# Low probabilities of a head's first 512 queries: from pairs of 64-column products to full products

## The chip, the core and the metric

The kernel runs on one core of a Trainium2 chip. The core has a matrix engine, TensorE (PE in the profile, with its weight loads shown as a row of their own, PEld), and four others: VectorE (DVE), ScalarE (ACT), GpSimd (POOL) and SyncE (SP), which here issues the DMAs. The metric is the time of one execution on the device, in microseconds (us); less is better. Beside the runs that are timed there is one execution taken by the profiler, from which all rows of the trace come.

## The reference

Two decoder layers over 1024 tokens of width 1024. Layer 0 mixes by causal pooling, layer 1 by attention with forget gates over 16 heads of 64 channels; both also attend to 256 memory tokens with 4 heads. The part that matters here is the attention of layer 1:

```python
def forgetting_attention(u, k, v, cum):
    ...
        logits = jnp.einsum('bqhd,bkhd->bhqk', qi, k,
                            preferred_element_type=jnp.float32) * scale
        logits = logits + (ci[..., :, None] - cum_k[:, :, None, :])
        ...
        logits = jnp.where(mask[None, None], logits, -jnp.inf)
        p = jax.nn.softmax(logits, axis=-1)
        return jnp.einsum('bhqk,bkhd->bqhd', p.astype(v.dtype), v)
```

All of it is float32. A query sees the keys up to its own place only, so with blocks of 128 the query block i needs i + 1 blocks of keys.

## The kernel before

TensorE is fed in 16-bit types or in a rounded form of float32, and the kernel keeps the accuracy by splitting numbers into a high and a low part. Products are then made of three: high with high, high with low, low with high. For the attention's values both probabilities and V are in float16: V of a head is stored as 128 columns for each block of 128 keys, 64 of its high part and 64 of its low part, and the probabilities, transposed, as one 128 x 128 block for each block of keys and part.

**fox()** runs the attention. Its outer loop goes over the 16 heads, two to a pair, its inner loop over the 8 blocks of 128 queries of a head, from the longest (i = 7) to the shortest. Each step does the following.

- `probs` (lines up to L1000): the products of queries and keys go to PSUM (written through the helper `mm3`, L231, into a bank of tag "L", of which there are 3). DVE adds the forget terms and keeps the running extreme (L986); POOL masks the diagonal block first (L978). ACT takes the exponential into a bank of tag "T", of which there are 2 (L994).
- `inverse_of` (L1004 to L1007): DVE forms one over the sum of a row.
- `halves` (L1015, L1016): ACT writes the high part of the scaled probabilities, DVE the low part.
- `turn` (L1028): a DMA on SP's queue transposes both parts into a tile of tag "T" in SBUF.
- `values` (L1034 to L1058): some steps later, once for the query blocks 4 to 7 (c = 1) and once for the blocks 0 to 3 (c = 0) of each head, the products with V. All four blocks of queries share one PSUM bank of 512 columns (tag "O", a single one).

Between these the helper `Fill` pumps in the products of other work (projections and gates of pairs to come: `slab`, L253, with PSUM banks of tag "pj"; toward the end the first part of the output projection, L540). How much is pumped where is counted in columns and shared out by step.

In `values`, the list `blocks` holds the pairs of a query block i and a key block j: 8 + 7 + 6 + 5 = 26 for c = 1, 4 + 3 + 2 + 1 = 10 for c = 0. A first loop (L1045) multiplies the 128 columns of V, high and low, with the high probabilities: rows 0 to 63 of the bank collect V's high part, rows 64 to 127 its low part. A second loop (L1051) multiplies V's high 64 columns alone with the low probabilities, by turns into the upper and the lower half of the bank, so that two successive products stand on different 64 columns of the array. At the end ACT (L1057) scales one half of the bank into the output tile and DVE (L1058) adds the other half, so it is the sum of both halves that counts, whichever half a term went to.

PE's instructions run in the order of the program, which is written out by hand (`tc.manual_schedule(engines={PE})`). The order on ACT, DVE, POOL and SP's queue is set by a planner when the kernel is built. It goes by modelled times and by what is ready; the program pins a few places with `tc.issue_after` and `tc.keep_in_program_order`.

After the last head, `out_proj.rest` (L540, with the splitting of its weights and inputs on ACT and DVE in `hi_lo`, L189 to L196) and the layer norm end the kernel.

Of the kernel before, what the change touches and what calls it, by code (L numbers as in the profile page):

```python
# [99 lines left out]
def trunk_kernel(ctx, tc, x, xT, memT, win, wk, wv0, wv, wmk, wmv, wout, poolw, pscale, lng, lnb, bforget, out):  # L100
# [5 lines left out]
    nc = tc.nc  # L106
# [22 lines left out]
    def ps(shape, tag, bufs):  # L129
        return psum.tile(shape, F32, tag=tag, name=nm(tag), bufs=bufs)  # L130
# [241 lines left out]
    def mem_attention(l, XH, XL, kv, qtile, ytile, yd):  # L372
# [85 lines left out]
        if True:  # L458
            for t in range(ST + 2):
                part = fill.left / (5 * (ST + 2 - t))  # L460
                if t < ST:
                    probs(t)
                fill.pump(part if t <= ST else 3 * part)
                for h in range(MH):
                    if t >= 3 and t % 2 == 1:
                        values((t - 3) // 2, h)
                    fill.pump(part if t <= ST else part / 2)
            fill.pump(float("inf"))
# [287 lines left out]
    with tc.tile_pool(name="in1", bufs=1) as in1:  # L756
# [262 lines left out]
        pt, homes = {}, {}  # L1019
# [14 lines left out]
        def values(hd, c, o):  # L1034


            (v, un), b = pairs[hd // 2][2], hd % 2
            acc = ps([P, NH], "O", 1)
            blocks = [(i, j) for i in range(4 * c + 3, 4 * c - 1, -1) for j in range(i + 1)]

            def cols(i):
                return slice((i % 4) * P, (i % 4 + 1) * P)

            for n, (i, j) in enumerate(blocks):
                nc.tensor.matmul(  # L1045
                    acc[:, cols(i)], v[:, b, 2 * j : 2 * j + 2, :].rearrange("p e d -> p (e d)"), pt[hd, i][:, j, :],
                    start=n == 0, stop=False, skip_group_check=True,
                )
            for n, (i, j) in enumerate(blocks):
                half = slice(64 * (n % 2), 64 * (n % 2) + 64)  # L1050
                nc.tensor.matmul(  # L1051
                    acc[half, cols(i)], v[:, b, 2 * j, :], pt[hd, i][:, i + 1 + j, :],
                    start=False, stop=n >= len(blocks) - 2, skip_group_check=True,
                )
            own, other = slice(64 * b, 64 * b + 64), slice(64 - 64 * b, P - 64 * b)
            oc = o[own, c * NH : (c + 1) * NH]
            nc.scalar.activation(oc, acc[other, :], AF.Copy, scale=un[own])  # L1057
            return nc.vector.scalar_tensor_tensor(oc, acc[own, :], un[own], oc, ALU.mult, ALU.add).ins  # L1058
# [30 lines left out]
        def fox(following, out_proj):  # L1089
# [8 lines left out]
            for hd in range(HEADS + 1):  # L1098
# [20 lines left out]
                for i in range(ST if hd < HEADS else LAG):  # L1119
# [46 lines left out]
                    if older and older[1] == (4 if older is past[0] else 0):  # L1166
                        last = values(older[0], older[1] // 4, older[2])
                        out_proj.behind = last if older[1] else out_proj.behind
                        if older[0] % 2 and older[1] == 0:
                            finished = pair_out(older[0] // 2, older[2], gs.get(older[0] // 2))  # L1170
# [83 lines left out]
```

## Time and profile before

| what | us |
|---|---|
| median of 3 runs | 1199.49 |
| lowest and highest run | 1198.80, 1199.53 |
| the profiled execution | 1198.79 |
| its span, first to last instruction | 1197.0 |
| mean granted clock of TensorE, share of full speed | 0.999 |

How to read the rows further down. A row of a source line gives the kind of instruction, the tiles (written <- read), a count, and durations as least, median and greatest in ns. A row of the timeline gives the start in us from the span's start, the length of the group in us, engine, line, operation, tiles, shapes, count, and in square brackets how long the engine was idle before it and what it was waiting for. A row of waits gives the engine and line that waited, the one that released it, the total in us, how often, and the longest. The engine named as releaser is inferred from the order of events; "issue" means that the profile shows nothing that was waited for. Ends of products on PE are modelled by the profiler, starts are recorded, and a product's recorded length contains its passage through the array, in which the next ones have already begun. A few per cent of the records of products can be missing.

### The profile page before, as it was taken

Reading aid. Unit: us, or ns where it says so; the run is one execution under the profiler, and the core shown is the slowest. Engines: PE = TensorE matmul, PEld = TensorE weight load, DVE = VectorE, ACT = ScalarE, POOL = GpSimd, SP = SyncE. Lnnn points to the kernel's source line nnn. Section 1 sums busy time; section 2 is a strip of 40 time slices with the busy share of each in tenths; the row PEclk is TensorE's granted clock in tenths of the full one; section 3 lists DMA queues with packets and bytes.
Section 4 is the critical chain, followed back from the end, with each engine's and each line's share of the span. In section 5 each row is a group of like instructions: output and inputs, shape, how many; then the busy total and the mean of one; then the engine's idle time right before and its main releaser. Section 6 shows DMA issues by size and latency. Waiting matters only on the chain. (4 is left out here: it accounts for less than half of the span.)

```text
span 1197.0 us, 19472 instructions
## 1 busy us (share of the span) xinstructions
PE 1172.2 (98%) x6810; PEld 739.3 (62%) x6927; DVE 800.5 (67%) x1864; ACT 616.9 (52%) x1330; POOL 208.4 (17%) x312
## 2 busy tenths in 40 slices
PE   9999999999999999999999999999999999999997
PEld 4567665555555555677776666666666666655554
DVE  6544767374656576377546888778878888874654
ACT  7433654262532224366325777767766787773110
POOL 2000000000000000200103334333334324530000
PEclk9999999999999999999999999999999999999999
DMA  7333654242355666355526789879897999976431
GB/s 246 115 101 87 131 115 159 79 123 80 102 197 158 159 156 161 106 138 100 171 54 161 152 199 173 195 155 195 187 186 164 195 191 210 230 206 229 154 116 48
DMA packets 280803, 182.06 MB, mean 152 GB/s; under 512 B 225024, under 2 KB 238976, under 8 KB 280704
## 3 DMA queue, kind: packets, MB, share of 16 engines
q1 hardware_dynamic: 280704, 180.81, 62.0%
q8 instruction: 54, 0.88, 0.3%
q14 instruction: 45, 0.37, 0.1%
HBM read 95.24 MB, written 22.61 MB: 98 GB/s over the span
## 5 line engine op out<-in xcount | busy, mean ns | idle before, releaser
L253 PE MATMUL pj<-A,w 128*128 128x512 bf16 (+1 forms) x1817 | 571.4, 398 | 2.2 <-DVE B L894 1.1
L253 PE MATMUL pj<-A,wl 128*128 128x512 bf16 x929 | 351.8, 380 | 6.4 <-issue 3.4
L253 PEld LDWEIGHTS pj<-A,w 128*128 128x128 f32 x944 | 174.8, 188 | 45.4 <-POOL wl L200 2.0
L253 PEld LDWEIGHTS <-w 128*128 128x128 bf16 x960 | 93.1, 98 | 121.3 <-issue 39.4
L253 PEld LDWEIGHTS <-wl 128*128 128x128 bf16 x960 | 94.3, 98 | 87.9 <-issue 4.2
L994 ACT ACTIVATE T<-MK,s 128x512 f32<-128x512 f32 x192 | 111.0, 578 | 44.5 <-DVE s L986 22.6
L1015 ACT ACTIVATE P<-T,s 128x512 f16<-128x512 f32 x192 | 103.1, 576 | 52.8 <-issue 26.3
L1016 DVE SCALAR_TENSOR_TENSOR P<-T,s,P 128x512 f16<-128x512 f32 x192 | 112.3, 612 | 24.0 <-ACT P L1015 22.3
L540 PEld LDWEIGHTS <-T 128*128 128x128 bf16 x736 | 70.6, 98 | 88.9 <-issue 6.8
L190 DVE TENSOR_TENSOR wl<-raw,w 128x512 bf16<-128x512 f32 (+1 forms) x96 | 67.9, 713 | 72.3 <-ACT w L189 69.7
L231 PE MATMUL L<-B,B 128*128 128x512 f32 (+3 forms) x384 | 109.0, 386 | 4.6 <-DVE s L986 4.2
L189 ACT CAST w<-raw 128x512 fp32r<-128x512 f32 (+1 forms) x104 | 62.8, 609 | 84.0 <-PE pj L253 57.6
L231 PEld LDWEIGHTS L<-B,B 128*128 128x128 f32 x384 | 71.1, 189 | 29.6 <-DVE s L986 9.9
L353 POOL TENSOR_SCALAR A<-A 128x1024 bf16<-128x1024 f32 x8 | 8.4, 1049 | 444.5 <-ACT A L351 427.9
L986 DVE CUSTOM_DVE_ANT_0 MK<-L,R 128x512 f32<-128x512 f32 (+3 forms) x128 | 72.8, 569 | 8.4 <-PE L L231 5.6
L978 POOL TENSOR_SCALAR_AFFINE_SELECT R<-R 128x128 f32<-128x128 f32 x128 | 42.2, 335 | 207.4 <-DVE s L986 162.5
L200 POOL TENSOR_TENSOR wl<-raw,w 128x512 bf16<-128x512 f32 x54 | 69.4, 1285 | 3.8
L190 DVE TENSOR_TENSOR T<-T,T 128x1024 bf16<-128x1024 f32 x23 | 31.6, 1374 | 48.1 <-ACT T L189 48.0
L189 ACT CAST T<-T 128x1024 fp32r<-128x1024 f32 x23 | 24.1, 1047 | 71.7 <-DMA T<-y1d 45.4
L199 POOL TENSOR_SCALAR w<-raw 128x512 fp32r<-128x512 f32 x54 | 35.9, 665 | 58.5 <-PE pj L253 58.5
L540 PE MATMUL L<-B,T 128*128 128x512 bf16 (+1 forms) x163 | 43.1, 391 | 0.3
L433 ACT ACTIVATE P<-L,s 128x256 f32<-128x256 f32 x64 | 29.6, 474 | 23.4 <-issue 13.0
(296 smaller groups left out, 1789.7 us busy)
## 6 DMA issues: line engine op xcount, KB each, us to landing
raw<-in_win_dram SPq DMA_DIRECT2D x94, 256.0 KB, 2.9
raw<-in_wout_dram SPq DMA_DIRECT2D x40, 256.0 KB, 2.9
B<-B SPq DMA_DIRECT2D x32, 256.0 KB, 4.5
R<-cumd SPq DMA_DIRECT2D x16, 512.0 KB, 4.6
T<-y0d SPq DMA_DIRECT2D x12, 512.0 KB, 5.1
y0d<-Y SPq DMA_DIRECT2D x11, 512.0 KB, 2.7
T<-y1d SPq DMA_DIRECT2D x11, 512.0 KB, 4.7
raw<-in_wmk_dram SPq DMA_DIRECT2D x16, 256.0 KB, 2.7
```

The costliest lines, as they stand in the source:

```text
L189: pin(nc.scalar.copy(hi, src))
L190: pin(by.tensor_tensor(lo[0], src, hi.bitcast(F32), ALU.subtract))
L199: nc.gpsimd.tensor_scalar(hi, src, 1.0, 1.0, ALU.mult, ALU.mult)
L200: nc.gpsimd.tensor_tensor(lo[0], src, hi.bitcast(F32), ALU.subtract)
L231: nc.tensor.matmul(acc, a, b, start=i == 0, stop=i == len(terms) - 1)
L253: nc.tensor.matmul(acc, a, b, start=start, stop=stop)
L540: nc.tensor.matmul(acc, y, w, start=c == 2 and j == firsts[id(acc)] and acc is not self.seeded, stop=c == 1 and j == lasts[id(acc)], skip_ ...
L978: nc.gpsimd.affine_select(R[:, qs], R[:, qs], [[-1, P]], ALU.is_ge, -NEG, base=0, channel_multiplier=1).ins
L986: nc.vector.tensor_tensor_reduce(p[:, lo:up], lg, R[:, lo:up], 1.0, top, ALU.add, ALU.min, m[:, n : n + 1])
L994: nc.scalar.activation(e, p[:, lo:up], AF.Exp, bias=top, scale=-1.0, accum_out=sums[:, n, hd % 2, i : i + 1],)
L1015: nc.scalar.activation(pair[:, lo:up], e, AF.Copy, scale=r)
L1016: nc.vector.scalar_tensor_tensor(pair[:, L + lo : L + up], e, r, pair[:, lo:up], ALU.mult, ALU.subtract)
```

## The change

For c = 0 the second loop takes V's high and low columns together, 128 of them, in place of the high 64 by turns on two halves of the array. Its products have the form of the first loop's, and the bank's closing mark is set on the last of them alone. For c = 1 nothing changes. The number of products is the same, 10 in each loop. The sum gains a term that was left out before, low probabilities with V's low part.

```diff
-            for n, (i, j) in enumerate(blocks):
+            if c == 0:
+                for n, (i, j) in enumerate(blocks):
+                    nc.tensor.matmul(
+                        acc[:, cols(i)], v[:, b, 2 * j : 2 * j + 2, :].rearrange("p e d -> p (e d)"),
+                        pt[hd, i][:, i + 1 + j, :], start=False, stop=n == len(blocks) - 1, skip_group_check=True,
+                    )
+            for n, (i, j) in enumerate(blocks if c else ()):
                 half = slice(64 * (n % 2), 64 * (n % 2) + 64)
                 nc.tensor.matmul(
                     acc[half, cols(i)], v[:, b, 2 * j, :], pt[hd, i][:, i + 1 + j, :],
```

## The prediction

> **What bounds the kernel now.** I read the page first: which engine is full, and by how much.
>
> ```profile
> span 1197.0 us, 19472 instructions
> PE 1172.2 (98%) x6810; PEld 739.3 (62%) x6927; DVE 800.5 (67%) x1864; ACT 616.9 (52%) x1330; POOL 208.4 (17%) x312
> ```
>
> TensorE (PE) is busy for 98% of the span. Time taken from it ought to come off the end, unless something else is as full where the change sits. So I asked for the busy time of the stretch in which the attention heads run, with the columns stretch, length, and busy time and count of PE, weight loads, DVE, ACT and POOL, then granted clock, DMA share and GB/s.
>
> ```profile
> 660.00:1060.00 400.00, 389.04 (x2629) 256.59 (x2674) 327.26 (x938) 292.68 (x679) 155.66 (x249) 1.00 0.92 188
> ```
>
> PE works 389 of these 400 us, DVE 327. That says PE. But the waits say something else. First what PE waited for from 655 to 1075 us, then what DVE waited for from 660 to 1060 (total, times, longest):
>
> ```profile
> PE L L231 <- DVE s L986: 4.2, 9, 1.0
> PE pj L253 <- issue: 3.8, 24, 0.2
> PE pj L253 <- DVE B L894: 1.1, 2, 0.5
> ```
>
> ```profile
> DVE P L1016 <- ACT P L1015: 22.0, 39, 1.1
> DVE s L1004 <- ACT T L994: 21.6, 25, 1.6
> DVE MK L986 <- PE L L231: 1.4, 4, 0.4
> ```
>
> DVE and ACT hand the softmax to and fro: DVE waits 22.0 and 21.6 us for ACT in these two groups, and only 1.4 us, in 4 places, for PE's logits (L231). PE in turn is held 9 times by DVE's reading of the logits (L986) and twice by DVE's reading of a projection (L894). So two chains run side by side, PE's and that of DVE with ACT, and each is sometimes ahead. Where in time they hold each other decides what a saving on PE is worth; that comes below.
>
> **The change, part by part.** It touches values() for c = 0 alone: 10 products with the low probabilities per head, 16 heads, 160 of the 576 products on L1051. All instances by shape:
>
> ```profile
> L1045 PEld LDWEIGHTS <-V x576: 96/98/100, 663.4 to 1069.0; 128*128 128x128 f16 x192
> L1045 PE MATMUL O<-T,V x576: 219/219/230, 663.6 to 1069.1; 128*128 128x128 f16 x192
> ```
>
> ```profile
> L1051 PEld LDWEIGHTS <-V x576: 106/110/110, 665.2 to 1069.4; 128*64 128x64 f16 x192
> L1051 PE MATMUL O<-T,V x576: 219/219/243, 665.2 to 1069.5; 128*64 128x128 f16 x192
> ```
>
> A product's 219 ns are its passage through the array; products overlap, so only spacings of starts count. The first c = 0 burst, the last but one, and for comparison a c = 1 burst (start, length of the group, product, count, idle before):
>
> ```profile
> 673.70 0.72 PE L1045 MATMUL O<-T,V 128*128 128x128 f16 x10
> 674.36 0.47 PE L1051 MATMUL O<-T,V 128*64 128x128 f16 x10
> 674.99 0.38 PE L253 MATMUL pj<-A,wl 128*128 128x512 bf16 x1 [0.16 <-issue]
> ...
> 1045.37 0.72 PE L1045 MATMUL O<-T,V 128*128 128x128 f16 x10
> 1046.02 0.47 PE L1051 MATMUL O<-T,V 128*64 128x128 f16 x10
> 1046.65 0.38 PE L253 MATMUL pj<-A,w 128*128 128x512 bf16 x1 [0.16 <-POOL R L1083]
> ```
>
> ```profile
> 663.63 1.61 PE L1045 MATMUL O<-T,V 128*128 128x128 f16 x26
> ```
>
> Removed: the halves. Ten of them are cheap in themselves: (0.47 - 0.22) / 9 = 28 ns from start to start, two of them in the time of one full product, which is (1.61 - 0.22) / 25 = 55.6 ns in the burst of 26. What is dear is getting in and out. The tenth full product starts at 673.70 + 9 x 0.0556 = 674.20, the first half only at 674.36: 0.16 us instead of 0.056, so 0.10 lost. The last half starts at 674.36 + 0.47 - 0.22 = 674.61, and the next ordinary product at 674.99: 0.38 us, where PE shows 0.16 idle after the half has left the array. The burst takes 674.99 - 673.70 = 1.29 us in all, 1.28 in the last but one; 15 of the 16 bursts have this form.
>
> The tiling page of the Trainium skill (TensorEngine Tiling (Array Packing), Key Properties) says that a change of tiling mode drains the array. The trace agrees: 0.10 us going in and 0.38 coming out.
>
> Added: 10 full products, so 20 in a row on one shape. Another place of this kernel has such a run without any halves behind it:
>
> ```profile
> 565.63 0.83 PE L231 MATMUL T<-T,MK 128*128 128x128 f16 x12
> 566.30 0.38 PE L253 MATMUL pj<-A,w 128*128 128x512 bf16 x1
> ```
>
> Twelve take 566.30 - 565.63 = 0.67 us up to the start of the next ordinary product, 55.8 ns each and nothing lost behind them. Twenty take 20 x 55.8 = 1.12 us. Against 1.28 that is 0.165 us less per burst (between 0.16 and 0.18 by 55.6 to 55.8 ns and 1.28 to 1.29 us), for 15 bursts 2.5 us. The loads of 128 columns (98 ns) are hidden already: the burst of 26 has one ahead of each product and still goes at 55.6. Dependences, counts of instructions, DMAs and tiles stay as they are, and the fill between the bursts is counted in columns that the change doesn't touch.
>
> The sixteenth burst is followed by f32 products that start before the halves have left:
>
> ```profile
> 1068.55 0.73 PE L1045 MATMUL O<-T,V 128*128 128x128 f16 x10
> 1069.21 0.47 PE L1051 MATMUL O<-T,V 128*64 128x128 f16 x10
> 1069.61 0.50 PE L540 MATMUL pj<-MK,B 128*128 128x512 f32 x1
> ```
>
> There it is 1.06 us before and 1.12 after; I take it as 0, with -0.06 as the bound.
>
> Moved: the sum in PSUM is finished later within a burst, at 19 x 0.0556 + 0.22 = 1.28 us after its start instead of 0.66 + 0.47 = 1.13. ACT reads it next (L1057); the burst with the least time between is this (PE, then ACT):
>
> ```profile
> 889.23 0.47 PE L1051 MATMUL O<-T,V 128*64 128x128 f16 x10
> ```
>
> ```profile
> 890.05 0.69 ACT L1057 ACTIVATE G<-O,unscale 64x512 f32<-64x512 f32 x1
> ```
>
> Before, the sum is there at 889.70, 0.35 ahead of ACT; 0.15 later still leaves 0.2. I cost it at nothing. Without that cover ACT's queue, with the next exponentials (L994) in it, would start up to 0.15 later.
>
> **Where the 2.5 us go.** Here are the places in time where PE is held by DVE, and then those where DVE's reading of the logits is held by PE.
>
> ```profile
> 687.66 0.62 PE L231 MATMUL L<-B,B 128*128 128x384 f32 x2 [0.83 <-DVE s L986]
> 749.96 0.47 PE L253 MATMUL pj<-A,w 128*128 128x512 f32 x1 [0.53 <-DVE B L894]
> 827.60 0.38 PE L231 MATMUL L<-B,B 128*128 128x256 f32 x1 [0.41 <-DVE s L986]
> 857.83 0.47 PE L253 MATMUL pj<-A,w 128*128 128x512 f32 x1 [0.53 <-DVE B L894]
> 1075.32 0.38 PE L540 MATMUL L<-MK,T 128*128 128x512 bf16 x1 [0.54 <-DVE MK L190]
> ```
>
> ```profile
> 780.12 0.69 DVE L986 CUSTOM_DVE_ANT_0 MK<-L,R 128x512 f32<-128x512 f32 x1 [0.28 <-PE L L231]
> 796.29 0.69 DVE L986 CUSTOM_DVE_ANT_0 MK<-L,R 128x512 f32<-128x512 f32 x1 [0.43 <-PE L L231]
> 887.96 0.69 DVE L986 CUSTOM_DVE_ANT_0 MK<-L,R 128x512 f32<-128x512 f32 x1 [0.25 <-PE L L231]
> 904.13 0.69 DVE L986 CUSTOM_DVE_ANT_0 MK<-L,R 128x512 f32<-128x512 f32 x1 [0.43 <-PE L L231]
> ```
>
> Follow the time. DVE with ACT sets the pace up to 749.96, where PE last waits for it. From there PE sets it, until DVE is short of logits at 780.12 and 796.29. Then DVE again, up to 857.83; PE up to 904.13; and from 904.13 on DVE isn't short of logits once, until PE waits at 1075.32 for weights that DVE splits. A PE that is 0.165 us early in a stretch that DVE paces only waits longer at that stretch's end. In PE's two stretches lie four bursts (751.65, 780.73, 859.53, 888.58): there the saving shortens DVE's waits of 0.28, 0.43, 0.25 and 0.43, which are larger than the 0.165 or 0.33 that arrives. Four times 0.165 is 0.66 us; the other eleven, 1.8 us, turn into waits on L986, L894 and L190.
>
> The profiled execution took 1198.79 us (its span of 1197.0 and 1.8 around it), 0.70 below the median of the runs, 1199.49. So 1198.79 - 0.66 = 1198.13 against the profiled one, and 1198.8 against the median. A measurement of this kernel can tell about 0.2%, 2.4 us, from no change, so this is no change.
>
> **Rivals.** All of the saving counts: PE is at 98%, the DVE waits at these places are short, and DVE's order in the stretch may have its own slack, a shorter PE giving it projections (L894, L905) earlier. Against it: DVE waits for PE in four places only. 1199.49 - 2.5 = 1197.0, or 0.21% faster, on the border of what can be told.
>
> The order on the other engines changes. PE's order is written out by hand, that of DVE, ACT, POOL and the DMA queue is worked out when the kernel is built, by a planner that goes by modelled times. If it prices full products unlike halves, near ties flip, and an operation put ahead of L1004 or L1016 makes DVE wait once more for ACT. The row of L1004 gives 21.6 / 25 = 0.86 us for such a wait. It decides where DVE paces, some 12 heads; one more in half of them costs 6 x 0.86 = 5.2, less 0.66: 1204.0. It takes four such waits (3.4 us) to be slower by more than can be told. For it: DVE is busy for 327 of 400 us there, and 25 waits of this kind stand already. Against it: same number of instructions and columns. The same flips could fall well: two waits less, with the 2.5, give 1195.3.
>
> Full products go at the pace of their loads: 98 ns instead of 55.8, 20 x 98 = 1.96 us a burst, 0.68 more than now, for 15 bursts 10.2: 1209.7. The burst of 26 at 55.6 is against it. The Trainium skill (TensorE: Matmul & The Clock Gate, Back-to-back issue gap) gives about 81 ns a product for a stream of pairs of load and product on 128 columns; by it 20 would take 1.62 us, 0.34 more than now, 16 x 0.34 = 5.4 in all, an estimate of 1204.9. This trace shows 55.6 for the same thing, and that decides.
>
> **How the numbers follow.** Forecast (part of the saving counts, order as before): 0.42. All of it counts: 0.20. Order changes: 0.36, of which 0.22 to the slower side, 0.14 to the faster. Pace of the loads: 0.02. Faster takes two thirds of the second case (0.14), the good flips (0.14) and a little of the forecast in which more bursts count than I found (0.08): 0.36. Slower is 0.22 and 0.02: 0.24. The rest, 0.40, is within 0.2%. The range goes from the good flips, 1195.3, to the bad ones, 1204.0; the forecast's own is 1197.0 to 1199.5.
>
> **What would show it.** In the changed profile a c = 0 burst should be one group of 20 products on 128 columns, 1.12 us to the next start, with no idle of 0.16 behind it; if it is near 1.6 or 2, the loads set the pace. DVE's waits for PE's logits should fall from 1.4 us, and PE's waits for L986 and L894 rise from 5.3 by about 1.8. If these stay and the span falls by 2.5, PE paced everywhere. If DVE's operations stand in another order around L1004, L1016 and L1058, the planner has moved, and the time is that of the new order. I am wrong if the time leaves 1197.0 to 1199.5 with the order unchanged.

## The result, and the profile after

The changed kernel takes 1201.61 us (median of 15 runs, 1200.93 to 1203.59) against 1199.39 for the kernel before beside it (15 runs, 1198.46 to 1199.91): a ratio of 1.0021, with a 95% interval from 1.0014 to 1.0029. That is 2.2 us slower: little, but the interval is clear of 1. The profiled execution took 1201.12 us.

The page of the kernel after, the span and the busy time of the engines:

```profile
span 1199.3 us, 19478 instructions
PE 1174.5 (98%) x6810; PEld 743.3 (62%) x6927; DVE 800.3 (67%) x1864; ACT 615.7 (51%) x1330; POOL 207.9 (17%) x312
```

The span is 2.3 us longer. Each engine has as many busy instructions as before, and DVE, ACT and POOL are as busy as before to within 1.2 us, so nobody got more work. The low products of c = 0 now stand on a line of their own, L1051 (c = 1 has moved to L1057, the two closing steps to L1063 on ACT and L1064 on DVE):

```profile
L1051 PE MATMUL O<-T,V x160: 219/219/219, 674.0 to 1071.8; 128*128 128x128 f16 x160
```

What PE waited for from 655 to 1080 us, and what DVE waited for from 660 to 1060 (total, times, longest):

```profile
PE L L231 <- DVE s L986: 6.2, 13, 1.3
...
PE pj L253 <- DVE B L894: 1.1, 2, 0.5
```

```profile
DVE P L1016 <- ACT P L1015: 25.1, 45, 1.1
...
DVE MK L986 <- PE L L231: 0.8, 2, 0.4
```

PE is held by DVE's reading of the logits for 6.2 us instead of 4.2. DVE waits for ACT's high halves in six more places (45 for 39), 3.1 us more in all. The change touches neither engine's work. The places where PE waits on L986 and did not before, from PE's timeline:

```profile
720.19 0.50 PE L231 MATMUL L<-B,B 128*128 128x256 f32 x2 [0.80 <-DVE s L986]
...
738.37 0.62 PE L231 MATMUL L<-B,B 128*128 128x384 f32 x2 [0.41 <-DVE s L986]
...
846.71 0.62 PE L231 MATMUL L<-B,B 128*128 128x384 f32 x2 [0.42 <-DVE s L986]
...
955.04 0.62 PE L231 MATMUL L<-B,B 128*128 128x384 f32 x2 [1.31 <-DVE s L986]
...
1005.05 0.62 PE L231 MATMUL L<-B,B 128*128 128x384 f32 x2 [0.43 <-DVE s L986]
```

(The wait at 955 is an older one that grew from 1.01.) PE's order is the same in both kernels, so the starts of its bursts of values can be compared one by one. The last two columns belong to the first two experiments below: the changed products in the order of before, and the products of before in the changed order. The execution of the last column was already 1.8 us late at the first burst (663.63), ahead of which no order differs; there only the steps count.

| burst starts before, us | after, minus before | changed products, order of before, minus before | products of before, changed order, minus before |
|---|---|---|---|
| 699.45 | -0.42 | -0.06 | +1.66 |
| 713.21 | -0.37 | 0.00 | +1.66 |
| 723.45 | +0.47 | -0.07 | +2.53 |
| 738.68 | +0.81 | -0.11 | +2.88 |
| 751.65 | +0.82 | -0.09 | +2.88 |
| 796.88 | +0.93 | +0.01 | +2.88 |
| 831.32 | +0.94 | +0.02 | +2.87 |
| 846.55 | +1.28 | -0.01 | +3.21 |
| 859.53 | +1.27 | -0.01 | +3.21 |
| 904.73 | +1.41 | +0.12 | +3.23 |
| 939.16 | +1.41 | +0.16 | +3.23 |
| 954.18 | +1.77 | +0.13 | +3.58 |
| 988.85 | +1.74 | +0.10 | +3.55 |
| 1004.08 | +2.09 | +0.09 | +3.90 |
| 1060.04 | +2.18 | +0.18 | +3.89 |

The loss comes in steps. One of 0.84 lies between 713 and 723, and four of 0.34 to 0.36 lie at 723 to 739, 831 to 847, 939 to 954 and 989 to 1004; together 0.84 + 0.34 + 0.34 + 0.36 + 0.35 = 2.23, nearly the whole loss. They are the five waits above. The last column has the same five steps (0.87, 0.35, 0.34, 0.35 and 0.35), with the products of before.

Comparing the order of the instructions on each engine shows what stands there. On DVE 19 small groups are in another order, on ACT two, on POOL one, on SP's queue four. Most of them form two patterns; what stands outside them (on DVE at 681, 760, 868 and 1053 us, on POOL at 971) has no step of more than 0.12 us beside it. The **first**, in four heads, is at the closing of c = 0. DVE's timeline before, and after:

```profile
727.36 0.56 DVE L986 CUSTOM_DVE_ANT_0 MK<-L,R 128x384 f32<-128x384 f32 x1
...
727.84 0.74 DVE L1058 SCALAR_TENSOR_TENSOR G<-O,unscale,G 64x512 f32<-64x512 f32 x1
728.51 0.99 DVE L1016 SCALAR_TENSOR_TENSOR P<-T,s,P 128x384 f16<-128x384 f32 x2
...
730.32 0.41 DVE L986 CUSTOM_DVE_ANT_0 MK<-L,R 128x256 f32<-128x256 f32 x1
```

```profile
727.81 0.56 DVE L986 CUSTOM_DVE_ANT_0 MK<-L,R 128x384 f32<-128x384 f32 x1
...
728.76 1.01 DVE L1016 SCALAR_TENSOR_TENSOR P<-T,s,P 128x384 f16<-128x384 f32 x2 [0.39 <-ACT P L1015]
729.69 0.73 DVE L1064 SCALAR_TENSOR_TENSOR G<-O,unscale,G 64x512 f32<-64x512 f32 x1
...
731.31 0.40 DVE L986 CUSTOM_DVE_ANT_0 MK<-L,R 128x256 f32<-128x256 f32 x1
```

Before, the closing step (L1058, 0.74 us) lay where DVE would have waited for ACT's high halves. After, it stands behind them (L1064): DVE idles 0.39 us first and does the step later, and the next reading of logits, which started 2.96 us after the first one (730.32 - 727.36), starts 3.50 after it (731.31 - 727.81). Of these 0.54 us some 0.34 reach PE 7 us later.

The **second** pattern occurs once, from 695 us on. DVE's timeline before, and after:

```profile
694.20 0.76 DVE L1058 SCALAR_TENSOR_TENSOR G<-O,unscale,G 64x512 f32<-64x512 f32 x1
694.99 0.69 DVE L986 CUSTOM_DVE_ANT_0 MK<-L,R 128x512 f32<-128x512 f32 x1
...
696.46 0.69 DVE L894 TENSOR_TENSOR B<-pj,B 64x512 fp32r<-64x512 f32 x1
697.18 0.56 DVE L986 CUSTOM_DVE_ANT_0 MK<-L,R 128x384 f32<-128x384 f32 x1
...
702.48 0.76 DVE L1058 SCALAR_TENSOR_TENSOR G<-O,unscale,G 64x512 f32<-64x512 f32 x1
```

```profile
694.56 0.69 DVE L986 CUSTOM_DVE_ANT_0 MK<-L,R 128x512 f32<-128x512 f32 x1
...
696.81 1.27 DVE L1016 SCALAR_TENSOR_TENSOR P<-T,s,P 128x512 f16<-128x512 f32 x2 [0.81 <-ACT P L1015]
698.12 0.68 DVE L894 TENSOR_TENSOR B<-pj,B 64x512 fp32r<-64x512 f32 x1
698.83 0.56 DVE L986 CUSTOM_DVE_ANT_0 MK<-L,R 128x384 f32<-128x384 f32 x1
...
702.96 0.76 DVE L1064 SCALAR_TENSOR_TENSOR G<-O,unscale,G 64x512 f32<-64x512 f32 x1
```

ACT's casts of a projection (L893) now stand behind its high halves (L1015) and its exponentials (L994), so DVE's L894, which needs the cast, and a reading of logits no longer fill DVE's wait for ACT. DVE, 0.43 us early at 694.56, is 0.48 late at 702.96, and PE meets that at 720.19.

### The profile page after: what moved, and what is told of

Read it like the earlier page. It is cut to its first block, busy times and chain, and to the rows that moved or that the text cites. A ratio compares the mean times of both kernels' runs of the same rounds, so it can differ in the third digit from the quotient of the medians.

```text
span 1199.3 us, 19478 instructions
## 1 busy us (share of the span) xinstructions
PE 1174.5 (98%) x6810; PEld 743.3 (62%) x6927; DVE 800.3 (67%) x1864; ACT 615.7 (51%) x1330; POOL 207.9 (17%) x312
## 5 line engine op out<-in xcount | busy, mean ns | idle before, releaser
L253 PE MATMUL pj<-A,w 128*128 128x512 bf16 (+1 forms) x1817 | 572.1, 399 | 1.6 <-DVE B L894 1.1
L253 PE MATMUL pj<-A,wl 128*128 128x512 bf16 x929 | 352.0, 380 | 5.4 <-issue 1.9
L253 PEld LDWEIGHTS pj<-A,w 128*128 128x128 f32 x944 | 174.9, 189 | 44.9 <-POOL wl L200 2.0
L253 PEld LDWEIGHTS <-w 128*128 128x128 bf16 x960 | 93.2, 98 | 121.0 <-issue 40.0
L253 PEld LDWEIGHTS <-wl 128*128 128x128 bf16 x960 | 94.4, 98 | 87.3 <-issue 4.0
L994 ACT ACTIVATE T<-MK,s 128x512 f32<-128x512 f32 x192 | 111.0, 578 | 45.8 <-DVE s L986 23.8
L1015 ACT ACTIVATE P<-T,s 128x512 f16<-128x512 f32 x192 | 103.1, 576 | 54.5 <-issue 27.8
L1016 DVE SCALAR_TENSOR_TENSOR P<-T,s,P 128x512 f16<-128x512 f32 x192 | 112.2, 612 | 27.1 <-ACT P L1015 25.4
L540 PEld LDWEIGHTS <-T 128*128 128x128 bf16 x736 | 70.5, 98 | 89.1 <-issue 6.9
L231 PE MATMUL L<-B,B 128*128 128x512 f32 (+3 forms) x384 | 109.0, 386 | 6.2 <-DVE s L986 6.2
L231 PEld LDWEIGHTS L<-B,B 128*128 128x128 f32 x384 | 71.1, 189 | 31.2 <-DVE s L986 11.5
L986 DVE CUSTOM_DVE_ANT_0 MK<-L,R 128x512 f32<-128x512 f32 (+3 forms) x128 | 72.7, 568 | 7.8 <-PE L L231 5.0
L540 PE MATMUL L<-B,T 128*128 128x512 bf16 (+1 forms) x163 | 43.2, 392 | 0.3
```

The source lines that it names most:

```text
L231: nc.tensor.matmul(acc, a, b, start=i == 0, stop=i == len(terms) - 1)
L253: nc.tensor.matmul(acc, a, b, start=start, stop=stop)
L540: nc.tensor.matmul(acc, y, w, start=c == 2 and j == firsts[id(acc)] and acc is not self.seeded, stop=c == 1 and j == lasts[id(acc)], skip_ ...
L986: nc.vector.tensor_tensor_reduce(p[:, lo:up], lg, R[:, lo:up], 1.0, top, ALU.add, ALU.min, m[:, n : n + 1])
L994: nc.scalar.activation(e, p[:, lo:up], AF.Exp, bias=top, scale=-1.0, accum_out=sums[:, n, hd % 2, i : i + 1],)
L1015: nc.scalar.activation(pair[:, lo:up], e, AF.Copy, scale=r)
```

## The experiments

To hold products and order apart, a kernel was given the recorded order of another. At the end of the program each engine's list of instructions (DVE, ACT, POOL, SP) is chained in the wanted order, as a constraint for the planner that needs no semaphore (NoSync); PE's order is written out by hand and stays. The code, shortened:

```python
for way in orders:                      # one list for each of DVE, ACT, POOL, SP
    for before, i in zip(way, way[1:]):
        tc.add_manual_dep(i, before.name, NoSync, reason="order")
```

All nine kernels compute the same attention (a full low product adds the term of low probabilities with V's low part); none leaves out work. Times are medians; a ratio, with its 95% interval, is against the kernel before run beside it.

### Products or order (the first two)

```diff
 e1: the changed kernel
+the order of before on DVE, ACT, POOL, SP
 e2: the kernel before
+the order of the changed kernel on DVE, ACT, POOL, SP
```

> The full products of the change, with every instruction of DVE, ACT, POOL and the DMA queue held in the order of the kernel before. Theory A, the planner's new order costs most of the 2.2 us and the products themselves 0.05 us a burst: 1199.4 to 1200.2, the waits of PE on L986 near 720, 738, 846 and 1005 us are gone again. Rival B, the products cost it all, whatever the order: 1201.6. The prediction's own sum (a burst saves 0.165 us): 1198.7.

> The pairs of halves as before, with the four other engines held in the order of the changed kernel. Theory A: 1201.0 to 1201.6, with PE's new waits on L986 at about 720 (0.8 us), 738, 846, 1005 (0.3 to 0.4 each) in place. Rival B: 1199.4, as before.

The changed products in the old order took 1199.21 us, a ratio of 1.0004 (0.9996 to 1.0013), just under the range expected. The old products in the changed order took 1201.41, a ratio of 1.0022 (1.0013 to 1.0031). The order carries the loss; the products by themselves can't be told from no change. That the second takes as long as the changed kernel (1201.61) says too that the chaining costs nothing that can be told. Its waits are close to those of the changed kernel, with the products of before (PE from 655 to 1080 us, DVE from 660 to 1060):

```profile
PE L L231 <- DVE s L986: 6.5, 12, 1.3
```

```profile
DVE P L1016 <- ACT P L1015: 25.1, 45, 1.1
```

In the first of the two, PE's waits from 655 to 1080, and the busy times on its page:

```profile
PE L L231 <- DVE s L986: 3.9, 9, 0.9
```

```profile
PE 1182.3 (99%) x6927; PEld 743.3 (62%) x6927; DVE 800.2 (67%) x1864; ACT 616.7 (51%) x1330; POOL 207.8 (17%) x312
```

PE waits nine times for L986, as before, and the steps of the table are gone. This trace has a record of a product for each of the 6927 weight loads, where those of before and after have 6810 products. That matters for the size of a burst, below.

### Which part of the order (two)

```diff
 e3: the changed kernel, its own order
+the first pattern (four heads) put back: closing step ahead of the low halves,
+with the reciprocals behind it and one transposing DMA each
 e4: the changed kernel, its own order
+the second pattern (one head) put back: casts ahead of the exponentials
```

> The changed kernel in its own order, but in four heads DVE's closing step of the values (the line after ACT's, 64x512), the reciprocals behind it and one transposing DMA each stand as before. Theory A puts 4 x 0.33 = 1.3 us on these four places: 1200.3, and PE's waits near 738, 846 and 1005 are gone while that near 720 stays. If only the other group counts, or the products: 1201.6.

> The changed kernel in its own order, but in one head (about 703 to 723 us) ACT's two casts of keys and DVE's steps around them stand as before. Theory A puts 0.84 us on this place: 1200.8, and PE's wait near 720 is gone while those near 738, 846 and 1005 stay. If only the four places of the values count, or the products: 1201.6.

With the first pattern put back the kernel took 1200.0 us, a ratio of 1.0011 (1.0002 to 1.0019); with the second, 1200.7, 1.0014 (1.0005 to 1.0023). From the change's 1.0021 that is 1.2 us for the four places and 0.8 us for the one, as the steps in the table have it (1.39 and 0.84); the intervals overlap, so it is the places in the traces that tell the two apart. PE's timeline with the first pattern back, and with the second:

```profile
720.23 0.51 PE L231 MATMUL L<-B,B 128*128 128x256 f32 x2 [0.80 <-DVE s L986]
...
737.16 1.51 PE L231 MATMUL L<-B,B 128*128 128x512 f32 x4
```

```profile
719.23 0.88 PE L231 MATMUL L<-B,B 128*128 128x384 f32 x4
...
737.80 0.61 PE L231 MATMUL L<-B,B 128*128 128x384 f32 x2 [0.46 <-DVE s L986]
```

Each takes away its own wait (a group of four without a pause where there were two and two) and leaves the other.

### How long a burst really is

The prediction's 1.29 us for a burst with halves doesn't fit the first experiment, where nothing was saved. The weight loads of before behind the burst that it read:

```profile
674.75 0.10 PEld L253 LDWEIGHTS <-w 128*128 128x128 bf16 x1
674.77 0.10 PEld L253 LDWEIGHTS <-wl 128*128 128x128 bf16 x1
674.99 0.10 PEld L253 LDWEIGHTS <-w 128*128 128x128 bf16 x1
```

Two loads start at 674.75 and 674.77, but the first product recorded is that at 674.99. A product with the first load's weights, begun at about 674.77, has no record. The "0.16 idle" is its time: 0.22 from start to start, of which the last half's passage covers 0.06. The same products and order with complete records are found in the kernel that follows (e6), in PE's timeline; behind it that of the first experiment:

```profile
673.65 0.72 PE L1045 MATMUL O<-T,V 128*128 128x128 f16 x10
674.30 0.47 PE L1051 MATMUL O<-T,V 128*64 128x128 f16 x10
674.70 0.39 PE L253 MATMUL pj<-A,w 128*128 128x512 bf16 x1
```

```profile
673.64 0.72 PE L1045 MATMUL O<-T,V 128*128 128x128 f16 x10
674.20 0.72 PE L1051 MATMUL O<-T,V 128*128 128x128 f16 x10
674.76 0.38 PE L253 MATMUL pj<-A,w 128*128 128x512 bf16 x1
```

The burst with halves takes 674.70 - 673.65 = 1.05 us, the one of twenty full products 674.76 - 673.64 = 1.12. The change makes a burst 0.07 us longer, not 0.165 shorter. (The rows are rounded; to the ns the bursts take 1.054 and 1.117 us, a difference of 0.063, in 15 of 16 heads.) In the trace of after the same gap in the records hides it: the first product recorded behind its bursts starts 1.33 us after the burst, the 1.12 and one product of 0.22 without a record.

### All low products full (one)

For c = 1 the difference is larger, so a cost on PE can be dosed with it.

```diff
-            if c == 0:
+            if True:
...
-            for n, (i, j) in enumerate(blocks if c else ()):
+            for n, (i, j) in enumerate(()):
+the order of before on DVE, ACT, POOL, SP
```

> Full products for c = 1 too, all four other engines in the order of before. Theory A reads one ordinary product of 0.216 us, of which the trace has no record, behind each burst of halves: 26 halves then take 1.08 - 0.22 = 0.86 us, 26 full ones 1.45, so 0.58 more a burst for c = 1 and 0.05 for c = 0: 16 x 0.63 = 10.1 on PE, less what PE now waits for DVE (about 3): 1206 to 1209. The prediction's reading (no such product; 1.08 against 1.45, and 0.165 saved for c = 0): 16 x 0.37 - 2.6 = 3.3 on PE at most: 1199 to 1202.5.

The first c = 1 burst in this kernel, and with halves in the kernel e6:

```profile
663.12 1.61 PE L1045 MATMUL O<-T,V 128*128 128x128 f16 x26
...
666.03 0.38 PE L253 MATMUL pj<-A,w 128*128 128x512 bf16 x1
```

```profile
663.65 1.61 PE L1045 MATMUL O<-T,V 128*128 128x128 f16 x26
...
666.04 0.39 PE L253 MATMUL pj<-A,w 128*128 128x512 bf16 x1
```

Full: 666.03 - 663.12 = 2.91 us; halves: 2.39. So 0.52 more for c = 1 and 0.07 for c = 0, to the ns 0.509 and 0.063: over 16 heads 16 x 0.57 = 9.2 us more work for PE (9.4 by the rounded rows, as an expectation below has it). The kernel took 1200.4 us, a ratio of 1.0012 (1.0004 to 1.0021): 1.4 us. The expectation from the full price, 1206 to 1209, missed by far. The time lies in the range given for the prediction's reading of the burst; it is the rows that speak against that reading. PE's wait for L986 in it:

```profile
PE L L231 <- DVE s L986: 0.9, 2, 0.6
```

The first experiment has the full products of c = 0 already, and both traces have a record of every product, in the same order. So the distance of each start from the one ahead of it can be compared product by product. The bursts of c = 1 are 8.1 us longer in all. The distances ahead of the logits' products (L231) are 5.7 us shorter, those ahead of the output projection's (L540) 0.9 and of the other projections' (L253) 0.5, which leaves 1.1 us at 1080 us (the ratios of the two kernels differ by 0.0008, 1.0 us). Of the 5.7 only 3.0 were recorded waits (3.9 less 0.9 above). The rest lay in pauses that show no idle time: a recorded product of 0.38 us starts 0.21 to 0.22 after the one ahead of it, so a pause of up to 0.16 between two such products stays hidden, as the missing product above has shown 0.16 for a gap of 0.38. So most of the added work went into pauses that PE had ahead of these products. That the hidden pauses too were waits for DVE is likely, but no row names what they waited for.

### DVE's closing step behind the logits (two)

DVE's waits showed a cheaper order too. In DVE's rows of before at 694.20, above, the closing step stands directly ahead of a reading of logits, for which PE waits at 695.74:

```diff
 e6: the kernel before, the order of before but for DVE, in 20 places:
-L1058 (closing step), L986 (reads logits)
+L986 (reads logits), L1058 (closing step)
 e7: the same order with the changed products
```

> The kernel before, its order held, but DVE's closing step of the values stands behind the next reading of logits (L986) in the 20 places where it stood directly ahead of it. Theory A (a DVE step of 0.75 us ahead of the L986 that PE waits for costs what PE waits): PE's waits of 0.65, 0.17, 0.41, 0.17, 0.41, 0.41 and 0.17 go, up to 2.4 us: 1196.6 to 1198.3. If DVE with ACT is the bound over each whole stretch and the place of one step doesn't matter: 1199.0.

> The same order as in the run before this one, with the full products of the change for c = 0. Theory A: PE paces more of the stretch now, so more of the 16 x 0.05 = 0.8 us shows: 0.3 to 0.8 above the run before. If a full burst were the cheaper one, as predicted: up to 2.5 below it.

The first took **1194.78 us**, a ratio of 0.9967 (0.9955 to 0.9979), more than expected and faster than both kernels. With the changed products it took 1195.1, 0.9969 (0.9957 to 0.9980), so full products bring nothing there either. PE's wait at that place in the timeline of before, and then DVE's and PE's rows there in e6:

```profile
695.74 0.50 PE L231 MATMUL L<-B,B 128*128 128x256 f32 x2 [0.65 <-DVE s L986]
```

```profile
694.07 0.68 DVE L986 CUSTOM_DVE_ANT_0 MK<-L,R 128x512 f32<-128x512 f32 x1
...
694.79 0.76 DVE L1058 SCALAR_TENSOR_TENSOR G<-O,unscale,G 64x512 f32<-64x512 f32 x1
```

```profile
694.59 0.74 PE L231 MATMUL L<-B,B 128*128 128x384 f32 x4
```

The bank of logits comes free 0.9 us earlier, and the same products go through in one group of four without a pause. Over the whole stretch the two kernels with the changed products and complete records (the first experiment and e7) can be compared as above: the distances ahead of L231 are 3.4 us shorter, 1.2 of it recorded waits, and the rest of the stretch changes by 0.2 in all. The closing step can wait: the next burst of values, which needs its bank, starts at 699.45, 5 us later.

### The two again, with DVE relieved; and one step too far

```diff
 e8: e6's order, all low products full (c = 0 and c = 1)
 e9: e6's order, and on DVE in 27 places:
-L284, L894 or L905 (reads a projection), L986 (reads logits)
+L986 (reads logits), L284, L894 or L905 (reads a projection)
```

> Full products for both c, in the order of the run that put DVE's closing step of the values behind the reading of logits (1194.8). The traces give a c = 1 burst 2.39 us with halves and 2.91 all full, and 1.05 against 1.12 for c = 0: 16 x 0.59 = 9.4 us on PE, of which only 1.4 showed in the time while DVE with ACT set the pace. Theory H: PE waits in pieces too short to be seen, since DVE paces; with DVE relieved of about 4 us more of the 9.4 shows: 1198 to 1203. Rival: the halves cost their neighbours what they save, so the full price is about 1.4 in any order: 1195.9 to 1196.6.

> The order of the run at 1194.8 and the products of before; DVE's reading of projections (L284, L894, L905), where it stands directly ahead of a reading of logits, goes behind it, in 27 places. If what PE waits for is always the next L986: 1192 to 1194.5. If PE then waits for its two banks of projections instead: 1195 to 1198.

e8 took 1199.06 us, a ratio of 0.9998 (0.9989 to 1.0007). Against e6 that is 0.0031 of 1199, 3.7 us, where the same 9.2 us of PE work cost 1.4 in the old order. The two prices differ by 2.3 us, just more than the intervals (1 to 1.4 us on each ratio) allow together. So with DVE relieved more of PE's work shows, as the expectation has it if DVE was the cover; the same small price in any order (1195.9 to 1196.6) didn't come. By the distances of the starts in the traces of e6 and e8, the bursts are 9.1 us longer, and the distances ahead of L231 are 3.1 us shorter, ahead of L253 1.5 and ahead of L540 0.4, from 655 to 1080 us.

e9 took 1197.69, 0.9984 (0.9975 to 0.9993): by the ratios 2.0 us slower than e6, a little more than the intervals can explain. PE's waits from 640 to 1080 in e9, and in e6:

```profile
PE L L231 <- DVE s L986: 2.9, 4, 1.3
PE pj L253 <- DVE B L894: 2.8, 3, 1.1
```

```profile
PE L L231 <- DVE s L986: 3.0, 4, 0.9
...
PE pj L253 <- DVE B L894: 0.4, 1, 0.4
```

The logits' waits don't fall any further, and the banks of projections (tag "pj") are now the late ones: 2.4 us more.

## Why the prediction was wrong

**The forecast, order as before, failed on its condition.** It was put at 0.42 against 0.36 for a new order. The order changed, and the second rival happened on its slower side: right in its mechanism (an operation that filled DVE's wait for ACT is moved, and DVE waits), too dear in its price. It put 6 waits at 0.86, the mean of L1004's. What came were six more waits of L1016, 3.1 / 6 = 0.52 us each, while L1004's waits stayed at 21.6 us in total, and five steps on PE, four of 0.34 to 0.36 and one of 0.84: 2.2 us instead of 5.2 less 0.66. The rule it named, other places around L1004, L1016 and L1058, was the one to look at. The forecast's step that failed is thus the order that it kept; with the order kept, the first experiment took 1199.21, inside its 1197.0 to 1199.5. Why the planner preferred the new order isn't in any trace.

**"The burst takes 1.29 us in all" was wrong, and with it the sign.** The step took the 0.16 of "issue" behind the halves for the array's drain. It was an unrecorded product. The prediction's own rows had two signs of it: 6810 products beside 6927 loads, and the sixteenth burst at 1.06, which it set aside as an exception and which was near the true size. With 1.05 the change adds 0.07 a burst.

What a halves burst costs follows from e6's rows. The first half starts 0.15 after the last full product (674.30 - 674.15, with 673.65 + 9 x 0.0556 = 674.15), where another full one would have started after 0.056. The next ordinary product starts 0.15 after the last half (674.70 - 674.55), where another half would have started after 0.028. So some 0.09 is lost going in and 0.12 coming out. The Trainium skill (TensorEngine Tiling (Array Packing), Key Properties) says that changing the tiling mode drains the array. The trace has a loss at each change, much less than the 0.38 that the prediction read coming out; that the array is empty in between it doesn't show, for the starts lie 0.15 apart and a product's recorded passage is 0.22. A half goes at 28 ns and a full product at 55.6, so a loss of 0.21 is earned back by about eight halves. By this ten gain some 0.06 and twenty-six some 0.5; the bursts show 0.07 and 0.52.

**"Twenty take 1.12 us" was right**, so the rival of the loads' pace (1.96) fell.

**"Four bursts in PE's two stretches count, the others are absorbed" fits the traces**, with the other sign. In the third column of the table the changed products lose 0.10 from 751.65 to 796.88 and 0.13 from 859.53 to 904.73, two bursts each, 0.06 a burst. That is the whole rise of the column from first to last (-0.06 to +0.18); elsewhere it goes up and down by up to 0.1 and nets nothing. The changed order with the two kinds of products (second column less last) rises by 0.11 and 0.12 in the same two stretches, and by 0.10 from 1004.08 to 1060.04, which the prediction didn't foresee. The prediction's sum with the true size, 4 x 0.06, gives +0.24 us; the first experiment's 1199.21 against 1198.95 agrees, though its ratio of 1.0004 would be 0.5 and the interval of about 1 us to each side allows much else. The rival "all of it counts" fell too: 9.2 us on all bursts cost 1.4.

**"Nothing for ACT's closing step, 0.2 to spare"** stands: the first experiment, with that step later in each burst, lost nothing beyond the four bursts.

**Two of the signs named would have misled.** PE's waits for L986 and L894 were to rise from 5.3 by about 1.8; they rose to 7.3, from the new order. DVE's waits for logits were to fall from 1.4; they fell to 0.8, since DVE had become late. Only with the order held do they speak of the products: in the first experiment PE's waits are 5.0 and DVE's 1.7, both moved as a longer burst would move them.

## What to carry to other kernels

Where a planner orders the other engines, an edit on one engine has two effects, its own and that of the new order; run the edit with the old order before explaining anything. Compare the count of products with that of weight loads, and look for two loads ahead of one product, before pricing a gap. Where the logits' banks hold PE, have the engine that frees them do it ahead of work whose bank isn't needed soon, and stop where the next kind of bank becomes the late one.

## What the runs showed of the hardware

Two successive products on different 64 columns go at 28 ns each, half the spacing of a full one, and against that spacing entering the form costs 0.09 us and leaving it 0.12: ten of them still win, by 0.06 us (a burst of 1.05 for one of 1.12). TensorE was shown busy for 98 to 99% of the span in all these kernels, yet 9.2 us of added products lengthened one of them by 1.4 and another by 3.7 us: a busy share near full does not mean that PE sets the time.
